# Tile 4 of both SwiGLU feed-forwards computed with seven block products in place of eight

## The chip, the cores and the metric

The kernel runs on 1 core of one Trainium2 chip. The metric is the device time of one execution in microseconds (us), lower is better. The kernel before takes 1363.11 us, the median of 3 runs (1362.15 to 1363.21).

## The reference

One hybrid decoder layer on 528 tokens (16 meta tokens and 512 of the sequence; the 112 empty ones ahead of them are masked), width 1024, in float32:

```
D_MODEL = 1024
D_FF = ((8 * D_MODEL // 3 + 127) // 128) * 128
def swiglu(x, w_in, w_out):
    a, b = jnp.split(x @ w_in, 2, axis=-1)
    return (jax.nn.silu(a) * b) @ w_out
...
    h = h + 0.5 * swiglu(rmsnorm(h, norm_ffn1), w_ffn1_in, w_ffn1_out)
    u = rmsnorm(h, norm_mix)
    fq, fk, fv, ff, rq, rk, rv, rg, ga, gb = jnp.split(u @ w_in, IN_SPLITS, axis=-1)
...
    mixed = g_a * (y_a @ w_o_fox) + g_b * (y_b @ w_o_ret)
    h = h + mixed @ w_out
    h = h + 0.5 * swiglu(rmsnorm(h, norm_ffn2), w_ffn2_in, w_ffn2_out)
```

D_FF is 2816, which is 22 inner tiles of 128 columns; each has a part a and a part b. Attention and retention, left out here, lie between the two feed-forwards.

## The kernel before, in words

Everything is kept transposed: channels on the 128 partitions, tokens along the free axis (528 in the first feed-forward, 512 in the second). A float32 product is made of three matmuls of split operands, high by high, high by low and low by high. `split` (L103) makes the two parts: ScalarE (ACT) copies the high part, VectorE (DVE) subtracts it from the source.

**The order of the feed-forward** is the string `SEQ` (L36), used twice by `ffn` (L369), once for each feed-forward. The tokens n0 and n1 are inner tiles 0 and 1, a2 b2, a3 b3 and a4 b4 are the two halves (a and b) of tiles 2, 3 and 4, each as plain products over all 1024 input channels (`mm3`, L289). From tile 5 on, e and l are the first four and the last three of seven block products, and p are the products with the output weights. The tokens u0 to u3 make sums of the normed input (`usums`, L348), on which these seven products rest: the tokens are cut into halves t1 and t2, the input channels into two halves of four chunks, the weights of a tile into a and b, and a 2 by 2 block product is made from seven products of blocks and of sums of blocks. `usums` leaves four pairs of tiles in `xa` and four in `xb`.

**TensorE (PE)** runs in the order in which the program issues (`manual_schedule`); the other engines' orders are set by a scheduler that knows priorities (`high_priority` for the epilogues of tiles below 4). All engines then run their list strictly in turn.

**A block product** (`prod`, L375) is 4 chunks of 3 matmuls, each with 264 columns in the first feed-forward and 256 in the second. With `onto=True` it adds to what its PSUM tile holds. `early` (L408) is such a use:

```
prod(b[0], w, 0, u, 0, t1)
nc.vector.tensor_tensor(cu[:, x1], b[0], R[:, t1], ALU.mult)
prod(b[1], v, 512, xa, 0, x2)
nc.vector.tensor_tensor(cu[:, x2], cu[:, x1], b[1], ALU.add)
prod(b[0], w, 512, u, 4, t1, True)
```

The third line of products adds to `b[0]`, so it can begin when DVE has read the first product out of it (L418). The four PSUM tiles of `pq` go round.

**Weights** go in pieces through `weights` (L231), four pieces ahead. A plain tile's piece (kind "w") is loaded twice by POOL's queue: once as the high part, then ACT writes its negative and a second load adds the weights to it (`ready`, L203). A tile of kind "S" is loaded whole by SP's queue into one of two raw buffers (`load`, L167); DVE makes the sums of its blocks with four operations (`wsums`, L181: L187 to L190) into the one buffer `ws`, and each piece A0, S0, A2 and S2 of raw weights or sums is split by ACT (L104) and DVE (L105).

**The epilogue** of a plain tile is `gated` (L390): three DVE operations of all tokens (L394, L397, L399), a Silu on ACT, and `store` (L384), a split. `early` and `late` have seven DVE operations of half the tokens, one of all, a Silu and `store`.

Of the kernel before, what the change touches and what calls it, by code (L numbers as in the profile page):

```python
# [19 lines left out]
AF = mybir.ActivationFunctionType  # L20
ALU = mybir.AluOpType
# [4 lines left out]
S = 512  # L26
# [6 lines left out]

SEQ = """n0 n1 a2 u0 b2 u1 a3 u2 b3 u3 a4 b4 e5 l5  # L36
          e6 p0 l6 p0 e7 p0 l7 p0 e8 p0 l8 e9 p0 l9 p0 e10 p0 l10
          e11 p1 l11 p1 e12 p1 l12 e13 p1 l13 p1 e14 p1 l14 e15 p1 l15 p1 e16 l16
          e17 p2 l17 p2 e18 p2 l18 p2 e19 p2 l19 p2 e20 p2 l20 e21 l21 p2 p3 p3 p3 p3 p3 p3 p3 p3""".split()
# [24 lines left out]
def layer(tc, order, hT, wf1i, wf1o, wf2i, wf2o, wmix, wsq, vecs, cs, rmask, rvec, cmask, outT):  # L64
    nc = tc.nc
    PSUM = bass.MemoryType.PSUM
    PE = mybir.EngineType.PE
    with ExitStack() as es:
# [18 lines left out]
        def ttile(name, dt=F32):  # L87
            return tp.tile([128, T], dt, name=name, tag="t", bufs=NT)
# [35 lines left out]
        loads = []  # L124
# [9 lines left out]
        def feed_ffn(seq, w_in, w_out):  # L134
            at_, nxt = {}, [0] * len(PJ)
            for tok in seq:
                c, j = tok[0], int(tok[1:])
                if c == "u":
                    continue
                if c == "p":  # L140
                    n = PJ[j] * 128
                    m = nxt[j]
                    nxt[j] += 1
                    if m % 2 == 0:
                        loads.append((w_out[j * 4 + m // 2], 2 * n, "w"))
                        at_[tok] = len(loads) - 1
                    pieces.append((at_[tok], m % 2 * n, n))
                    continue
                if c in "nae":
                    loads.append((w_in[j], 2048, "S" if c == "e" else "w"))  # L150
                    at_[j] = len(loads) - 1
                cuts = {"n": [0, 1024], "a": [0], "b": [1024],
                        "e": ["A0", "S0"], "l": ["A2", "S2"]}[c]
                pieces.extend((at_[j], x, 512 if x == "S2" else 1024) for x in cuts)

        feed_ffn(SEQ, wf1i, wf1o)
        for i in range((NMIX + 1) // 2):
# [5 lines left out]
        u = [], []  # L163
# [67 lines left out]
        def weights():  # L231
            i = at["u"]
            at["u"] += 1
            begin(i + 6)
            ready(i + 4)
            assert i in got
            return got.pop(i)
# [45 lines left out]
        R = cp.tile([128, T], F32, name="R")  # L283
# [85 lines left out]
        def ffn(seq, u, gain, a, pst, pq, norm, done, name):  # L369
            rng = rng_(a)  # L370
            o = po_(a)
            nh, t1, t2, x1, x2 = halves(a)
            xs = xa, xb = ([], []), ([], [])
            Rv = R[:, a:T]
            def prod(out, w, off, x, k0, ts, onto=False):  # L375


                for k in range(4):
                    c = slice(off + 128 * k, off + 128 * k + 128)
                    mm3s(out, [z[:, c] for z in w], [z[k0 + k][:, ts] for z in x], not onto and k == 0, k == 3, onto)  # L380

            g = {}

            def store(j, sv):  # L384
                xh = atile(f"{name}gh{j}", F32R)
                xl = atile(f"{name}gl{j}", F32R)
                split(xh[:, a:T], xl[:, a:T], sv)
                g[j] = xh, xl

            def gated(j, pa, pb):  # L390
                with tc.high_priority(offset=HF if j < 4 else 0):
                    sv = ttile(f"{name}s{j}")
                    for ps, x, y in pa:
                        nc.vector.tensor_tensor(sv[:, x:y], ps, R[:, x:y], ALU.mult)  # L394
                    sv = sv[:, a:T]
                    nc.scalar.activation(sv, sv, AF.Silu)
                    nc.vector.tensor_tensor(sv, sv, Rv, ALU.mult)  # L397
                    for ps, x, y in pb:
                        nc.vector.tensor_tensor(sv[:, x - a:y - a], sv[:, x - a:y - a], ps, ALU.mult)  # L399
                    store(j, sv)  # L400

            def whole(ps):
                return [(ps[:, o + a:o + T], a, T)]

            def singles(n):
                return [(pq(f"{name}{n}_{x}")[:, :y - x], x, y) for x, y in rng]

            def early(j):  # L408


                b = [pq(f"{name}q{j}_{x}")[:, :nh] for x in range(3)]
                cu = ttile(f"{name}cu{j}")[:, :2 * nh]
                d = ttile(f"{name}d{j}")[:, :nh]
                sv = ttile(f"{name}s{j}")[:, :2 * nh]
                w = weights()
                v = weights()
# [5 lines that stand above are left out]
                nc.vector.tensor_tensor(sv[:, x1], b[0], R[:, t1], ALU.mult)  # L422
                prod(b[2], v, 0, xa, 0, x1)
                nc.vector.tensor_tensor(d, cu[:, x2], b[2], ALU.add)
                return cu, d, sv

            def late(j, cu, d, sv):
                b = [pq(f"{name}r{j}_{x}")[:, :nh] for x in range(2)]
                bv = ttile(f"{name}b{j}")[:, :2 * nh]
                w = weights()  # L430
                v = weights()
                prod(b[0], w, 0, xb, 0, x1)
                nc.vector.tensor_tensor(bv[:, x2], d, b[0], ALU.add)
                prod(b[1], v, 0, u, 4, t2)
                nc.vector.tensor_tensor(sv[:, x2], b[1], R[:, t2], ALU.mult)
                nc.vector.tensor_tensor(sv[:, x2], sv[:, x2], d, ALU.add)
                nc.scalar.activation(sv, sv, AF.Silu)
                prod(b[0], w, 512, xb, 0, x2, True)
                nc.vector.tensor_tensor(bv[:, x1], cu[:, x2], b[0], ALU.add)
                nc.vector.tensor_tensor(sv, sv, bv, ALU.mult)  # L440
                return sv

            half, nxt = {}, [0] * len(PJ)
            for tok in seq:
                c, j = tok[0], int(tok[1:])
                if tok == "n0":
                    pa0, pb0 = pst(f"{name}pa0"), pst(f"{name}pb0")
                    for _ in zip(mm3(views(pa0, o, rng), weights(), u, KC), mm3(views(pb0, o, rng), weights(), u, KC)):
                        pass

                    first = []
                    for n, ps in (("sa", pa0), ("sb", pb0)):
                        sv = ttile(f"{name}{n}0")
                        nc.scalar.activation(sv[:, a:T], ps[:, o + a:o + T], AF.Copy)
                        first.append([(sv[:, a:T], a, T)])
                elif tok == "n1":
                    pa, pb = singles("pa1"), singles("pb1")
                    run(mm3(pa, weights(), u, KC))
                    norm(pa0, pb0)
                    gated(0, *first)  # L460
                    run(mm3(pb, weights(), u, KC))
                    gated(1, pa, pb)
                elif c == "u":
                    usums(j, gain, a, xs, name)
                elif c == "a":
                    half[j] = pst(f"{name}pa{j}")
                    run(mm3(views(half[j], o, rng), weights(), u, KC))
                elif c == "b":
                    pb = pst(f"{name}pb{j}")
                    run(mm3(views(pb, o, rng), weights(), u, KC))  # L470
                    gated(j, whole(half[j]), whole(pb))
                elif c == "e":
                    half[j] = early(j)
                elif c == "l":
                    store(j, late(j, *half[j]))
                else:
                    m = nxt[j]
                    nxt[j] += 1
                    js = range(sum(PJ[:j]), sum(PJ[:j + 1]))
                    x = [[g[x][i] for x in js] for i in range(2)]  # L480
                    w = weights()

                    end = a and j == len(PJ) - 1 and m == KC - 1
                    for z in ([(a, a + nh), (a + nh, T)] if end else [(a, T)]):
                        po = pst(f"{name}po{j}_{m}_{z[0]}")
                        run(mm3(views(po, o, [z] if end else rng), w, x, PJ[j]))
                        done(j, m, po[:, o + z[0]:o + z[1]], *z)
# [39 lines left out]
        u = nu  # L527
# [10 lines left out]
        with tc.tile_pool(name="psM", bufs=1, space=PSUM, reuse_waits="tile") as pM:  # L538
# [576 lines left out]
            u = [], []  # L1115
            for m in range(KC):
                x = atile(f"hh{m}")
# [130 lines left out]
```

## Time and profile before

| what | value |
|---|---|
| median of 3 runs | 1363.11 us |
| the profiled execution | 1366.41 us |
| its span, first to last instruction | 1364.3 us |
| mean granted clock of TensorE | 0.999 |
| PE busy, share of the span | 99% |
| weight loads of PE | 90% |
| DVE | 61% |
| ACT | 48% |
| POOL | 22% |
| matmuls | 8959 |
| DMA | 217.56 MB, mean 159 GB/s |

The profiled execution is one run, taken with the profiler; its span leaves out 2.1 us around the instructions. A matmul of PE is shown with its whole length though the next one starts within it, so that the distance of two starts tells what one costs. The same holds of DVE and ACT, whose next operation starts a little before the last one's end. The share of an engine over the whole span says little of one stretch.

### The profile page before, as it was taken

The numbers are of one execution on the slowest core, as the hardware profiler recorded it, in microseconds if no ns is written. First come the engines' busy times: TensorE is split into PE (matmuls) and PEld (weight loads), VectorE is DVE, ScalarE is ACT, GpSimd is POOL, SyncE is SP. The second block draws the span as 40 slices with busy tenths as digits, with TensorE's granted clock in tenths as the row PEclk, the third lists the DMA queues.
The fourth block names the chain that finished last, engine by engine and source line by source line (L and its number), as shares of the span: only waits on it lengthen the run. The fifth ranks groups of instructions, "written<-read, shape, count | busy, mean of one in ns | idle before, by whom it ended". The sixth has DMA issues, their size and how long they took to land.

```text
span 1364.3 us, 22600 instructions
## 1 busy us (share of the span) xinstructions
PE 1346.6 (99%) x8959; PEld 1229.1 (90%) x8959; DVE 836.3 (61%) x1711; ACT 657.9 (48%) x1059; POOL 300.5 (22%) x436
## 2 busy tenths in 40 slices
PE   9999999999999999999999999999999999999999
PEld 8999999999988788888888899888887999998997
DVE  6976777766455665556654565523337766777662
ACT  7433333333477677777744444453436333343331
POOL 2011111112433322333321211323421011111121
PEclk9999999999999999999999999999999999999999
DMA  9554444454996757776776766889976445555546
GB/s 295 122 143 123 127 129 118 132 143 92 288 222 140 182 130 156 169 169 149 168 179 129 149 143 141 201 228 239 268 175 124 132 131 128 134 147 133 146 90 167
DMA packets 64248, 217.56 MB, mean 159 GB/s; under 512 B 7680, under 2 KB 8064, under 8 KB 59664
## 3 DMA queue, kind: packets, MB, share of 16 engines
q0 software_dynamic: 51904, 166.91, 55.2%
q1 hardware_dynamic: 12096, 49.18, 9.9%
q8 instruction: 70, 1.15, 0.3%
q14 instruction: 34, 0.28, 0.1%
q10 hardware_dynamic: 144, 0.04, 0.0%
HBM read 207.68 MB, written 8.42 MB: 158 GB/s over the span
## 4 chain that ended last, share of the span: by engine, by line
PE 85%; issue 4%; DVE 4%; ACT 3%; POOL 2%; DMA 2%; SPq 0%; POOLq 0%; ACTq 0%
PE spo L297 9%; PE fq L307 7%; PE sq L307 7%; PE fpo L297 7%; PE pg L297 6%; PE sr L307 5%; PE fr L307 5%; PE prv L297 3%; PE oa L297 3%; PE prg L297 3%; PE ow L297 3%; PE ob L297 3%; PE pq L297 3%; PE pk L297 3%; PE fpb L297 2%
## 5 line engine op out<-in xcount | busy, mean ns | idle before, releaser
L228 ACT ACTIVATE wl<-wh 128x1024 fp32r<-128x1024 f32 (+2 forms) x169 | 160.7, 951 | 123.5 <-PE prg L297 25.0
L104 ACT ACTIVATE wh<-w 128x1024 fp32r<-128x1024 f32 (+1 forms) x74 | 76.7, 1036 | 195.7 <-issue 68.4
L104 ACT ACTIVATE wh<-ws 128x1024 fp32r<-128x1024 f32 x68 | 57.2, 841 | 99.8 <-PE fr L307 22.5
L105 DVE TENSOR_TENSOR wl<-w,wh 128x1024 fp32r<-128x1024 f32 (+1 forms) x74 | 88.0, 1189 | 6.1 <-ACT wh L104 6.1
L229 POOL DMA_DIRECT2D wl<-in_wmix x65 | 57.2, 880 | 116.4 <-ACT wl L228 98.5
L201 POOL DMA_DIRECT2D wh<-in_wmix x65 | 37.6, 579 | 183.5 <-PE pg L297 37.2
L297 PE MATMUL fpo<-fgh,wh 128*128 128x272 f32 x352 | 71.4, 284 | 0.0
L297 PE MATMUL fpo<-fgl,wh 128*128 128x272 f32 x352 | 71.3, 284 | 0.0
L297 PE MATMUL fpo<-fgh,wl 128*128 128x272 f32 x352 | 71.2, 284 | 0.0
L297 PE MATMUL spo<-sgh,wh 128*128 128x512 f32 (+1 forms) x181 | 70.2, 388 | 0.0
L297 PE MATMUL spo<-sgl,wh 128*128 128x512 f32 (+1 forms) x181 | 70.1, 387 | 0.0
L297 PE MATMUL spo<-sgh,wl 128*128 128x512 f32 (+1 forms) x181 | 70.0, 387 | 0.0
L105 DVE TENSOR_TENSOR wl<-ws,wh 128x1024 fp32r<-128x1024 f32 x68 | 64.6, 950 | 0.2 <-ACT wh L104 0.2
L105 DVE TENSOR_TENSOR pl<-PT,ph 128x512 fp32r<-128x512 f32 (+4 forms) x80 | 33.7, 432 | 48.1 <-ACT ph L104 47.6
L229 POOL DMA_DIRECT2D wl<-in_wf1o x32 | 28.2, 882 | 138.8 <-ACT wl L228 74.7
L229 POOL DMA_DIRECT2D wl<-in_wf2o x32 | 28.0, 876 | 134.9 <-ACT wl L228 70.5
L1143 DVE SCALAR_TENSOR_TENSOR hh<-spo,hh 128x512 f32<-128x512 f32 (+1 forms) x33 | 22.3, 675 | 57.8 <-PE spo L297 57.8
L297 PE MATMUL pg<-n2uh,wh 128*128 128x512 f32 x128 | 54.3, 424 | 0.0
L297 PEld LDWEIGHTS fpo<-fgh,wh 128*128 128x128 f32 x352 | 54.0, 188 | 0.0
L297 PEld LDWEIGHTS fpo<-fgl,wh 128*128 128x128 f32 x352 | 53.9, 188 | 0.0
L297 PEld LDWEIGHTS fpo<-fgh,wl 128*128 128x128 f32 x352 | 53.8, 188 | 0.0
L820 ACT ACTIVATE P<-P,st 128x144 f32<-128x144 f32 (+1 forms) x64 | 36.6, 571 | 30.7 <-DVE st L816 29.3
(959 smaller groups left out, 4665.2 us busy)
## 6 DMA issues: line engine op xcount, KB each, us to landing
wh<-in_wmix POOLq DMA_DIRECT2D x65, 512.0 KB, 4.9
wl<-in_wmix POOLq DMA_DIRECT2D x65, 512.0 KB, 7.1
w<-in_wf1i SPq DMA_DIRECT2D x18, 1024.0 KB, 7.4
w<-in_wf2i SPq DMA_DIRECT2D x17, 1024.0 KB, 7.5
wh<-in_wsq POOLq DMA_DIRECT2D x24, 512.0 KB, 5.2
wl<-in_wsq POOLq DMA_DIRECT2D x24, 512.0 KB, 7.7
wh<-in_wf1o POOLq DMA_DIRECT2D x16, 384.0 KB, 3.9
wl<-in_wf1o POOLq DMA_DIRECT2D x16, 384.0 KB, 5.3
```

What stands on the lines that cost most here:

```text
L104: nc.scalar.activation(xh, src, AF.Copy)
L105: nc.vector.tensor_tensor(xl, src, f32(xh), ALU.subtract)
L201: nc.gpsimd.dma_start(high[i][:, :w], loads[li][0][:, c:c + w])
L228: nc.scalar.activation(wl[:, :w], f32(wh[:, :w]), AF.Copy, scale=-1.0)
L229: nc.gpsimd.dma_start(wl[:, :w], raw[li][:, c:c + w], accum_op=ALU.add)
L297: nc.tensor.matmul(out, p[:, o:o + 128], q[:, a:b], start=first and k == 0 and i == 0, stop=last and k == nk - 1 and i == 2)
L307: nc.tensor.matmul(out, p, q, start=start and i == 0, stop=stop and i == 2, skip_group_check=onto)
L820: last["exp"] = nc.scalar.activation(P[i][:, :w], P[i][:, :w], AF.Exp, scale=-1.0, bias=st[:, 2:3], accum_out=sm[:, 0:1])
L1143: nc.vector.scalar_tensor_tensor(h[m][:, x:y], ps, 0.5, h[m][:, x:y], ALU.mult, ALU.add)
```

## The change

Tile 4 of both feed-forwards, computed until now by a4 and b4, becomes one token f4, with the seven block products. `foremost` issues all seven in a new order, the three that use no sums of tokens first: two of them on `u` with A0 and S2, the third with A0 again, onto `b[0]`. Then come the products with `xa` and `xb`; `b[1]` is used by three of them, the last one onto it. Tile 4's weights become kind "S" with the pieces in the order A0, S2, S0, A2. The rest of the program is as it was, but the scheduler sets the engines' orders anew.

```diff
-SEQ = """n0 n1 a2 u0 b2 u1 a3 u2 b3 u3 a4 b4 e5 l5
+SEQ = """n0 n1 a2 u0 b2 u1 a3 u2 b3 u3 f4 e5 l5
...
-                if c in "nae":
-                    loads.append((w_in[j], 2048, "S" if c == "e" else "w"))
+                if c in "naef":
+                    loads.append((w_in[j], 2048, "S" if c in "ef" else "w"))
                     at_[j] = len(loads) - 1
                 cuts = {"n": [0, 1024], "a": [0], "b": [1024],
-                        "e": ["A0", "S0"], "l": ["A2", "S2"]}[c]
+                        "e": ["A0", "S0"], "l": ["A2", "S2"], "f": ["A0", "S2", "S0", "A2"]}[c]
...
+            def foremost(j):
+
+                b = [pq(f"{name}q{j}_{x}")[:, :nh] for x in range(4)]
...
+                w = weights()
+                prod(b[0], w, 0, u, 0, t1)
+                nc.vector.tensor_tensor(cu[:, x1], b[0], R[:, t1], ALU.mult)
+                prod(b[1], weights(), 0, u, 4, t2)
+                nc.vector.tensor_tensor(sv[:, x2], b[1], R[:, t2], ALU.mult)
+                prod(b[0], w, 512, u, 4, t1, True)
+                nc.vector.tensor_tensor(sv[:, x1], b[0], R[:, t1], ALU.mult)
+                v = weights()
+                prod(b[2], v, 512, xa, 0, x2)
+                nc.vector.tensor_tensor(cu[:, x2], cu[:, x1], b[2], ALU.add)
+                w = weights()
+                prod(b[1], w, 0, xb, 0, x1)
+                bv = ttile(f"{name}b{j}")[:, :2 * nh]
+                nc.vector.tensor_tensor(bv[:, x2], cu[:, x2], b[1], ALU.add)
+                prod(b[3], v, 0, xa, 0, x1)
+                nc.vector.tensor_tensor(d, cu[:, x2], b[3], ALU.add)
+                nc.vector.tensor_tensor(bv[:, x2], bv[:, x2], b[3], ALU.add)
+                nc.vector.tensor_tensor(sv[:, x2], sv[:, x2], d, ALU.add)
+                nc.scalar.activation(sv, sv, AF.Silu)
+                prod(b[1], w, 512, xb, 0, x2, True)
+                nc.vector.tensor_tensor(bv[:, x1], cu[:, x2], b[1], ALU.add)
+                nc.vector.tensor_tensor(sv, sv, bv, ALU.mult)
+                return sv
...
+                elif c == "f":
+                    store(j, foremost(j))
```

Where the order of DVE changes. In the kernel before, this stands on DVE ahead of the first read of a block product (the last row, tile 5 of the first feed-forward; `fs_903` is tile 4's epilogue, `ws_924` the sums of tile 6's weights):

```order
L394 TENSOR_TENSOR fs_903<-fpa_797,R 128x528
L105 TENSOR_TENSOR wl_919<-ws_714,wh_798 128x512
L187 TENSOR_TENSOR ws_924<-w_712 128x512
L397 TENSOR_TENSOR fs_903<-fs_903,R 128x528
L188 TENSOR_TENSOR ws_924<-ws_924,w_712 128x512
L189 TENSOR_TENSOR w_712<-w_712 128x512
L190 TENSOR_TENSOR ws_924<-w_712,ws_924 128x512
L399 TENSOR_TENSOR fs_903<-fs_903,fpb_850 128x528
L105 TENSOR_TENSOR wl_929<-w_712,wh_851 128x1024
L105 TENSOR_TENSOR fgl_909<-fs_903,fgh_908 128x528
L418 TENSOR_TENSOR fcu_915<-fq_0_912,R 128x264
```

In the changed kernel the first read of a block product is that of tile 4, and tile 5's weights have their sums made right behind it (`fxbl_792` is the last of what u3 makes; `ws_822` are the sums of tile 5, `fq_0_795` and `fq_1_796` are `b[0]` and `b[1]` of tile 4):

```order
L105 TENSOR_TENSOR wl_803<-w_422,wh_645 128x1024
L105 TENSOR_TENSOR fxbl_792<-fxb_782,fxbh_791 128x528
L451 TENSOR_TENSOR fcu_799<-fq_0_795,R 128x264
L187 TENSOR_TENSOR ws_822<-w_559 128x512
L105 TENSOR_TENSOR wl_827<-w_559,wh_716 128x1024
L188 TENSOR_TENSOR ws_822<-ws_822,w_559 128x512
L189 TENSOR_TENSOR w_559<-w_559 128x512
L190 TENSOR_TENSOR ws_822<-w_559,ws_822 128x512
L453 TENSOR_TENSOR fs_801<-fq_1_796,R 128x264
L455 TENSOR_TENSOR fs_801<-fq_0_795,R 128x264
```

The first read of `b[0]` stands directly behind the whole of u3, and the read of `b[1]` (L453) behind the four sums and one split of tile 5's weights. Further on, this stands on DVE between tile 4's last product and tile 5's first read (`ws_937` are the sums of tile 6, `fgl_922` is tile 4's `store`):

```order
L466 TENSOR_TENSOR fs_801<-fs_801,fd_800 128x264
L105 TENSOR_TENSOR wl_932<-ws_822,wh_856 128x512
L469 TENSOR_TENSOR fb_889<-fcu_799,fq_1_796 128x264
L187 TENSOR_TENSOR ws_937<-w_820 128x512
L470 TENSOR_TENSOR fs_801<-fs_801,fb_889 128x528
L188 TENSOR_TENSOR ws_937<-ws_937,w_820 128x512
L189 TENSOR_TENSOR w_820<-w_820 128x512
L105 TENSOR_TENSOR fgl_922<-fs_801,fgh_921 128x528
L190 TENSOR_TENSOR ws_937<-w_820,ws_937 128x512
L105 TENSOR_TENSOR wl_942<-w_820,wh_873 128x1024
L418 TENSOR_TENSOR fcu_928<-fq_0_925,R 128x264
```

Tile 6's sums, tile 4's last two operations with its `store`, and the split of tile 6's first piece now stand between tile 4's last read of `b[1]` (L469) and tile 5's first read (L418); before, one split and one `store` stood between tile 4's last operation (L399) and that read.

## Rows read from the trace of the kernel before

**Rows 1.** The page, part 1: busy time, share of the span, instructions.
```profile
PE 1346.6 (99%) x8959; PEld 1229.1 (90%) x8959; DVE 836.3 (61%) x1711; ACT 657.9 (48%) x1059; POOL 300.5 (22%) x436
```

**Rows 2.** Windows: length, busy PE, PEld, DVE, ACT, POOL; granted clock; DMA.
```profile
44.00:56.00 12.00, 12.00 (x101) 12.00 (x101) 12.00 (x22) 5.35 (x8) 0.88 (x1) 1.00 0.28 46
446.20:449.60 3.40, 3.40 (x11) 2.73 (x10) 2.79 (x5) 2.35 (x5) 1.53 (x3) 0.50 0.92 217
1045.00:1057.00 12.00, 12.00 (x53) 9.72 (x52) 11.86 (x22) 4.94 (x8) 0.42 (x1) 1.00 0.12 24
```

**Rows 3.** Waits of PE: us in total, times, longest us.
```profile
PE k2pm L661 <- ACT k2sh L104: 2.1, 1, 2.1
PE sq L307 <- DVE scu L418: 1.6, 1, 1.6
PE fq L307 <- DVE fcu L418: 1.4, 1, 1.4
```

**Rows 4.** Timeline of PE, both feed-forwards: start, length, what.
```profile
56.23 0.41 PE L297 MATMUL fpa<-n1uh,wh 128*128 128x272 f32 x2
...
67.91 0.28 PE L307 MATMUL fq<-n1uh,wh 128*128 128x264 f32 x1
...
69.37 0.29 PE L307 MATMUL fq<-fxah,wh 128*128 128x264 f32 x1
...
70.96 0.39 PE L307 MATMUL fq<-n1uh,wh 128*128 128x264 f32 x1
...
1056.34 0.40 PE L297 MATMUL spa<-n3uh,wh 128*128 128x512 f32 x1
...
1067.50 0.29 PE L307 MATMUL sq<-n3uh,wh 128*128 128x256 f32 x1
...
1068.93 0.28 PE L307 MATMUL sq<-sxah,wh 128*128 128x256 f32 x1
...
1070.52 0.39 PE L307 MATMUL sq<-n3uh,wh 128*128 128x256 f32 x1
```

**Rows 5.** Timeline of DVE, first feed-forward.
```profile
32.24 0.71 DVE L394 TENSOR_TENSOR fs<-fsa,R 128x528 f32<-128x528 f32 x1
...
39.08 0.71 DVE L105 TENSOR_TENSOR fgl<-fs,fgh 128x528 fp32r<-128x528 f32 x1 [1.21 <-ACT fgh L104]
...
56.05 0.77 DVE L355 SCALAR_TENSOR_TENSOR fbk<-h,VEC,R 128x528 f32<-128x528 f32 x1
56.73 0.43 DVE L358 TENSOR_TENSOR fxa<-fbc 128x264 f32<-128x264 f32 x1
57.08 0.43 DVE L360 TENSOR_TENSOR fxb<-fbk,fbc 128x264 f32<-128x264 f32 x1
...
57.77 1.22 DVE L105 TENSOR_TENSOR wl<-ws,wh 128x1024 fp32r<-128x1024 f32 x1
58.90 0.70 DVE L399 TENSOR_TENSOR fs<-fs,fpb 128x528 f32<-128x528 f32 x1
59.52 0.43 DVE L361 TENSOR_TENSOR fxb<-fbk,fxa 128x264 f32<-128x264 f32 x1
...
70.48 0.43 DVE L418 TENSOR_TENSOR fcu<-fq,R 128x264 f32<-128x264 f32 x1
```

**Rows 6.** Timeline of DVE, second feed-forward.
```profile
1033.36 0.69 DVE L394 TENSOR_TENSOR ss<-ssa,R 128x512 f32<-128x512 f32 x1
...
1053.13 0.69 DVE L105 TENSOR_TENSOR sxbl<-sxb,sxbh 128x512 fp32r<-128x512 f32 x1
1053.73 1.22 DVE L105 TENSOR_TENSOR wl<-w,wh 128x1024 fp32r<-128x1024 f32 x1
1054.87 0.74 DVE L355 SCALAR_TENSOR_TENSOR sbc<-hh,VEC,R 128x512 f32<-128x512 f32 x1
1055.53 0.74 DVE L355 SCALAR_TENSOR_TENSOR sbk<-hh,VEC,R 128x512 f32<-128x512 f32 x1
```

**Rows 7.** The page, part 6: DMA issues, KB each, us to landing.
```profile
w<-in_wf1i SPq DMA_DIRECT2D x18, 1024.0 KB, 7.4
```

More of the change, by code (lines that the diff above doesn't have):

```diff
@@ L441, in late @@
                 return sv
+            def foremost(j):
+                b = [pq(f"{name}q{j}_{x}")[:, :nh] for x in range(4)]
+                cu = ttile(f"{name}cu{j}")[:, :2 * nh]
+                d = ttile(f"{name}d{j}")[:, :nh]
+                sv = ttile(f"{name}s{j}")[:, :2 * nh]
+                w = weights()
[21 more added lines that the diff above has]
+                return sv
             half, nxt = {}, [0] * len(PJ)
```

## The prediction

> **What bounds the kernel now.** I read the page's shares first: PE is busy 99% of the span and DVE 61% [rows 1]. So a us in which PE stands is a us of the result, and matmuls saved are us saved, as long as PE is fed. Then the windows around the place: in both feed-forwards DVE is as full as PE there, 12.00 of 12 us in the first and 11.86 in the second [rows 2], because u0 to u3 are made there beside the epilogues of tiles 0 to 3. ACT has 5.35 and 4.94 of 12 us to do. Last the waits of PE: one of 1.4 and one of 1.6 us already come from exactly the read that the change puts there, L418, which takes a block product out of its PSUM tile before the next product adds to it [rows 3]. So the question is not how many matmuls go, but when DVE gets to these reads.
>
> **What PE saves.** In the first feed-forward a4 begins at 56.23 us and tile 5 at 67.91: tile 4 takes 11.68 us. A product takes 69.37 - 67.91 = 1.46 us; seven are 10.22, so 1.46 are saved. In the second: 1067.50 - 1056.34 = 11.16; a product takes 1.43, with the start that I round to 1.42; seven are 9.94, so 1.22 are saved [rows 4]. Together 2.68 us, if PE waits for nothing.
>
> **What DVE gets to do.** Cost per operation, start to start [rows 5]: 0.68 us for L355 (56.05 to 56.73), 0.345 for half the tokens, 1.14 for a split of 1024 (57.77 to 58.90), 0.62 for all tokens (58.90 to 59.52). In the second [rows 6]: 0.60 for 512, 1.14, and 0.66 for L355; 0.34 for 256. Per tile 4 the change adds to DVE three and a half splits of weights (3 x 1.14 + 0.60 = 4.0 us) and four sums (2.4), which POOL's loads did so far; its epilogue goes from three operations of all tokens to eight of half and one of all, 1.6 us more. It takes nothing away from DVE. ACT exchanges two casts of 1024 for four splits: in the windows above it has the time, so nothing. SP loads 1 MB more for each feed-forward, POOL four pieces fewer.
>
> **The first read.** Product 2 takes `b[1]`, product 3 adds to `b[0]`, so it must wait until L451 has read `b[0]`. In the order shown with the change, L451 stands behind all of u3. From the first operation after the norm (L394 at 32.24 [rows 5]) DVE has ahead of it: 22 operations of all tokens (8 splits in `usums`, 14 of epilogues), two pairs of pieces of tile 1 at 0.68 a pair, 8 of L355, 16 of half, three splits of 1024 and one of 512 of tile 4's weights. That is 13.64 + 1.36 + 5.44 + 5.52 + 3.42 + 0.60 = 29.98 us, so L451 starts at 62.22. It takes 0.43, and 0.05 later PE can go on (before: a read at 70.48 of 0.43, PE at 70.96 [rows 4, 5]): 62.70. PE is done with products 1 and 2 at 56.23 + 2.92 = 59.15. **Wait 3.55 us.**
>
> **The next two.** Product 4 needs no new buffer; PE ends it at 65.62. Product 5 overwrites `b[1]`, whose read L453 stands behind L451, one sum, one split of 1024 and three more sums: 62.22 + 0.345 + 0.60 + 1.14 + 1.80 = 66.10, and 0.48 later PE starts, at 66.58. **Wait 0.96.** Product 6 ends at 69.50. Product 7 adds to `b[1]` behind L462; up to it DVE has three halves and two splits of 1024, 3.32 us, so it starts at 69.42 and PE at 69.90. **Wait 0.40.** Product 7 ends at 71.36.
>
> **The wait in tile 5.** Tile 5's third product adds to its `b[0]` behind L418. L469 can start with the end of product 7's last matmul, 71.24 + 0.28 = 71.52; then DVE has, as the last order shown says, 0.345, one sum, L470, two sums, the split of the `store`, a sum and a split of 1024: 5.12 us. L418 starts at 76.65, PE at 77.13. Two products after 71.36 PE would be there at 74.28. **Wait 2.85.** Before, this product started at 70.96 [rows 4]. So the first feed-forward loses 77.13 - 70.96 = **6.17 us**, and from there on DVE keeps up as before: nothing is added to later tiles.
>
> **The second feed-forward**, by the same steps from 1033.36 [rows 6]: 24 operations of 512 (the last split of u3 stands behind the read here), 8 of L355, 16 of 256, three splits: 14.52 + 5.28 + 5.41 + 3.42 = 28.63; read at 1061.99, PE on at 1062.46 instead of 1059.18: wait 3.28. L453 at 1066.47, behind that split too; product 5 at 1066.94 instead of 1065.30: 1.64. Product 7 at 1070.24 instead of 1069.78: 0.46; its end 1071.66. L469 at 1071.82, 5.08 us to L418, PE at 1077.37 instead of 1074.50: 2.87. Before, it was 1070.52 [rows 4]: **6.85 us** lost. Sum of both: **13.0 us**.
>
> **The clock.** [...] Bounds: 0, and 0.3 + 1.7 + 1.7 = 3.7 us. I take 1.7, one stretch that counts, since one row at 2.1 us shows that it happens and none that it must.
>
> [...]
>
> **What is covered.** Tile 6's weights are loaded into the raw buffer of tile 4, free when A2 is split at about 61.6 us; 7.4 us later [rows 7] they are there, 69.0, and their first sum is due at 71.9. That cover is 2.9 us; a load later than that would move L418 by as much.
>
> **Sum.** 13.0 + 1.7 = 14.7 us. The profiled execution took 1366.41 us with a span of 1364.3; it would take 1381.1 and 1379.0. The median of the runs shown is 3.3 us lower, so the forecast is 1363.11 + 14.7 = **1377.8 us**. A measurement of this kernel tells about 0.2%, 2.7 us, from no change.
>
> **The rivals.** *PE decides* (4%): the seven products go through without a wait, and 2.7 us are saved: 1360.4. For it speaks that PE is the fullest engine [rows 1]. It decides if L451 could start by 58.7, 3.5 us sooner than I count; against it, DVE had no free time in which to catch up [rows 2].
> [...]
>
> *Only tile 4 waits* (10%): DVE reaches L418 in time, because the scheduler's queue of 5.1 us meets operands that are there, and the 2.85 and 2.87 are not paid: 13.0 - 5.7 = 7.3, 1370.4 us. It would need DVE to save 2.9 of 5.1 us; nothing in the rows is that much faster.
>
> *More than the walk* (10%): ACT's splits come late. Before, DVE stood for one of them for 1.21 us at 39.08 [rows 5]; if each feed-forward loses 1 us more in this way and the clock its 3.7, it is 13.0 + 2.0 + 3.7 = 18.7: 1381.8. Against it: the casts of tile 4's pieces (L228), for which ACT has to await POOL's loads, are among what the change takes away.
>
> *Nothing to be seen* (4%): PE's waits are half of what I count, and the saving meets them: 1363 to 1366.
>
> **The numbers.** The forecast's own case has 72%, 1376.1 (no clock) to 1379.8 (all of it). With the second and third rival the range is 1370.4 to 1381.8 and leaves out some 8%, and as much again for what the walk misses. Faster 0.04, same 0.04, slower 0.92.
>
> **What would show it.** PE's waits for L451 and L453 of 3 to 4 and 1 to 2 us in each feed-forward, and for L418 in tile 5 of about 2.9; PE at 98% or less; DVE without a gap from 40 to 71 us; tile 6 beginning about 6 and 13 us later than before; half clock after some of these waits. I am wrong if the third product of tile 4 starts right after the second, or if L418 in tile 5 isn't waited for.

## The result, and the profile after

The changed kernel takes **1380.76 us**, the median of 3 runs (1377.57 to 1382.90), against 1363.11: 17.7 us more, a ratio of 1.0123 with a 95% interval of 1.0108 to 1.0139. The profiled execution is the fastest of the three, 1377.57 us with a span of 1375.7; the other two had spans of 1378.8 and 1381.0 at mean granted clocks of 0.995 and 0.993 instead of 0.998.

Part 1 of the page after, the line that answers to [rows 1]:

```profile
PE 1345.6 (98%) x8983; PEld 1230.3 (89%) x8983; DVE 852.5 (62%) x1741; ACT 661.8 (48%) x1063; POOL 296.3 (22%) x428
```

PE is busy 1.0 us less than before, a smaller share of a longer span; DVE is busy 16.2 us more. Where PE stood, by its waits (us in total, times, longest), beside [rows 3]:

```profile
PE sq L307 <- DVE scu L418: 4.4, 2, 2.8
PE fq L307 <- DVE fcu L418: 4.3, 2, 2.9
PE fq L307 <- DVE fcu L451: 3.7, 1, 3.7
PE sq L307 <- DVE scu L451: 3.4, 1, 3.4
...
PE k2pm L693 <- ACT k2sh L104: 1.4, 1, 1.4
```

`fq` is a product's PSUM tile in the first feed-forward, `sq` in the second. Four waits are new: for L451 at tile 4 and for L418 at tile 5, each once in both. The smaller waits for L418 of before (1.4 and 1.6) are still in the totals: they stand at a much later tile, at 249 and 1243 us of the kernel before. Tile 5's read was not waited for there. The two in the first feed-forward, in PE's timeline (start, us, operation, in brackets the idle time ahead and what ended it):

```profile
63.08 0.42 PE L307 MATMUL fq<-n1uh,wh 128*128 128x264 f32 x1 [3.67 <-DVE fcu L451]
...
77.99 0.40 PE L307 MATMUL fq<-n1uh,wh 128*128 128x264 f32 x1 [2.89 <-DVE fcu L418]
```

DVE meanwhile, in its timeline; [rows 5] are its operations in the same place before. No idle time stands in a bracket until the fourth row, and it is the only one between 42 and 78 us:

```profile
62.60 0.42 DVE L451 TENSOR_TENSOR fcu<-fq,R 128x264 f32<-128x264 f32 x1
...
66.49 0.42 DVE L453 TENSOR_TENSOR fs<-fq,R 128x264 f32<-128x264 f32 x1
...
69.78 0.42 DVE L462 TENSOR_TENSOR fb<-fcu,fq 128x264 f32<-128x264 f32 x1
...
70.75 0.43 DVE L464 TENSOR_TENSOR fd<-fcu,fq 128x264 f32<-128x264 f32 x1 [0.56 <-PE fq L307]
...
77.51 0.43 DVE L418 TENSOR_TENSOR fcu<-fq,R 128x264 f32<-128x264 f32 x1
```

And the clock, in windows (their length, then PE, PEld, DVE, ACT and POOL busy, then the granted clock, the DMA share and GB/s):

```profile
56.00:60.00 4.00, 3.41 (x29) 3.20 (x27) 4.00 (x9) 1.26 (x2) 0.00 (x0) 1.00 0.00 0
60.00:64.00 4.00, 0.92 (x5) 0.92 (x6) 4.00 (x7) 0.67 (x2) 0.00 (x0) 0.91 0.21 49
64.00:68.00 4.00, 4.00 (x24) 4.00 (x24) 4.00 (x7) 2.53 (x3) 0.56 (x1) 0.66 0.63 247
68.00:72.00 4.00, 4.00 (x35) 4.00 (x34) 3.44 (x8) 1.10 (x2) 0.00 (x0) 1.00 0.49 124
...
76.00:80.00 4.00, 2.01 (x16) 2.01 (x17) 2.60 (x5) 0.00 (x0) 0.00 (x0) 1.00 0.00 0
80.00:86.00 6.00, 6.00 (x51) 6.00 (x50) 3.94 (x8) 2.43 (x3) 1.68 (x3) 1.00 0.40 86
...
1064.00:1068.00 4.00, 0.97 (x4) 0.98 (x5) 4.00 (x8) 1.26 (x2) 0.00 (x0) 0.85 0.24 70
1068.00:1072.00 4.00, 4.00 (x26) 3.84 (x25) 4.00 (x8) 2.00 (x3) 0.55 (x1) 0.72 0.56 222
```

From 60 to 64 us PE ran 5 matmuls, from 64 to 68 it ran 24 where 35 is usual: half clock, right behind the wait. A second such stretch follows the wait for L451 at 1067. None follows the two waits for L418: the clock is 1.00 from 76 to 86 us, and from 1080 to 1088. Tile 6 of the first feed-forward begins at 85.42 instead of 78.38, 7.0 us late; in the second the lateness grows from 4.3 to 11.6, by 7.3. Between them 3.5 us come back at 446: PE's wait for ACT is 1.4 there instead of 2.1 [rows 3], a wait of 0.8 for DVE ahead of it is gone, and so is the half-clock stretch of before [rows 2], with a clock of 1.00 from 440 to 460 us; 0.8 go to a wait for ACT ahead of that (`pff`, 1.1 instead of 0.3). 7.0 + 0.8 - 3.5 + 7.3 = 11.6, close to the 11.4 by which the profiled spans differ.

### The profile page after: what moved, and what is told of

It reads as the page before. It is cut to its first block, busy times and chain, and to the rows that moved or that the text cites. A ratio compares the mean times of both kernels' runs of the same rounds, so it can differ in the third digit from the quotient of the medians.

```text
span 1375.7 us, 22681 instructions
## 1 busy us (share of the span) xinstructions
PE 1345.6 (98%) x8983; PEld 1230.3 (89%) x8983; DVE 852.5 (62%) x1741; ACT 661.8 (48%) x1063; POOL 296.3 (22%) x428
## 4 chain that ended last, share of the span: by engine, by line
PE 78%; DVE 9%; ACT 5%; issue 4%; DMA 2%; POOL 1%; SPq 0%; POOLq 0%; ACTq 0%; DVEq 0%
PE spo L297 9%; PE fq L307 7%; PE sq L307 7%; PE fpo L297 7%; PE pg L297 5%; PE sr L307 5%; PE fr L307 5%; PE prv L297 3%; PE oa L297 3%; PE prg L297 3%; PE ow L297 3%; PE ob L297 3%; PE pq L297 3%; PE pk L297 3%; PE prk L297 2%
## 5 line engine op out<-in xcount | busy, mean ns | idle before, releaser
L228 ACT ACTIVATE wl<-wh 128x1024 fp32r<-128x1024 f32 (+2 forms) x165 | 156.5, 949 | 115.4 <-PE prg L297 25.0
L104 ACT ACTIVATE wh<-w 128x1024 fp32r<-128x1024 f32 (+1 forms) x78 | 80.9, 1038 | 197.6 <-issue 68.7
L104 ACT ACTIVATE wh<-ws 128x1024 fp32r<-128x1024 f32 (+1 forms) x72 | 60.6, 842 | 104.3 <-PE fr L307 21.4
L105 DVE TENSOR_TENSOR wl<-w,wh 128x1024 fp32r<-128x1024 f32 (+1 forms) x78 | 92.9, 1191 | 6.2 <-ACT wh L104 6.2
L105 DVE TENSOR_TENSOR wl<-ws,wh 128x1024 fp32r<-128x1024 f32 (+1 forms) x72 | 68.4, 950 | 0.2 <-ACT wh L104 0.2
L201 POOL DMA_DIRECT2D wh<-in_wf1o x32 | 19.9, 622 | 148.6 <-PE fq L307 68.3
```

Source lines behind the costliest of these rows:

```text
L104: nc.scalar.activation(xh, src, AF.Copy)
L105: nc.vector.tensor_tensor(xl, src, f32(xh), ALU.subtract)
L201: nc.gpsimd.dma_start(high[i][:, :w], loads[li][0][:, c:c + w])
L228: nc.scalar.activation(wl[:, :w], f32(wh[:, :w]), AF.Copy, scale=-1.0)
```

## The experiments

Theory 1 is the prediction's: DVE has more to do ahead of the reads than it has time for, and PE stands until it gets there. Rival 2: the reads only stand badly in DVE's list. Rival 3: PE itself (matmuls, weights). Rival 4: the clock. Each run's time stands beside runs of the kernel before on the same chip.

**One feed-forward at a time.** The token f4 is put back to a4 b4 in the second, then in the first:

```diff
+SEQB = " ".join(SEQ).replace("f4", "a4 b4").split()
-        feed_ffn(SEQ, wf2i, wf2o)
+        feed_ffn(SEQB, wf2i, wf2o)
...
-            ffn(SEQ, u, gn2, NM, psB, pqB, norm2, done2, "s")
+            ffn(SEQB, u, gn2, NM, psB, pqB, norm2, done2, "s")
```

> The first feed-forward has f4, the second a4 b4 as before. Theory 1 (DVE has more to do than it has time for ahead of the reads of tile 4 and 5, and PE waits for it): in the changed kernel tile 6 of the first feed-forward began 85.42 - 78.38 = 7.0 us later, 3.5 of which were given back at 446 us, where a half-clock stretch of before is gone; so 3.5 to 7 us above the kernel before, 1366.6 to 1370.2 us, and the first feed-forward's waits as in the changed kernel (L451 3.7, L418 2.9 us). Rival (the two places share a cause outside them, such as the loads of weights or PE's clock over the whole span): most of the 17.7 us or next to nothing of them.

> The second feed-forward has f4, the first a4 b4 as before. Theory 1: the changed kernel's second tile 5 ended 7.3 us later than before by itself (4.26 to 11.56 us in the shift of PE), so 1370.4 us, give or take 2, with waits of 3.4 (L451) and 2.8 us (L418) there and the first feed-forward as before. What this run and the one with the first alone lose should add up to the loss of the changed kernel, 17.7 us, within 4. Rival (a shared cause): they do not add up.

The first alone: 1370.83 against 1363.85 us, 1.0051 (1.0036 to 1.0066). The second alone: 1371.09, 1.0063 (1.0046 to 1.0079). That is 7.0 and 7.2, together 14.2 of 17.7, within the 4 allowed. The first is 0.6 us above the top of its expectation (1370.2, reckoned from 1363.11; the runs of the kernel before beside it are 0.7 higher). The two places lose apart from each other, and each shows its own two waits (3.7 and 2.9, 3.4 and 2.8).

**DVE's new work alone, on the eight products of before.**

```diff
-                    loads.append((w_in[j], 2048, "S" if c == "e" else "w"))
+                    loads.append((w_in[j], 2048, "S" if c == "e" or tok == "a4" else "w"))
...
+                cuts = {"a4": ["A0", "S2", "S0"], "b4": ["A2"]}.get(tok, cuts)
...
+                    if j == 4:
+                        weights()
+                        weights()
```

(One of the sums, which would overwrite raw weights, goes to a place that nothing uses.)

> The kernel before, with a4 and b4 as plain products of eight, but tile 4's weights come as in the change: SP loads them whole, DVE makes the four sums and ACT and DVE split all four pieces (two of the pieces are used by nothing). So DVE has 4.0 + 2.4 = 6.4 us more per feed-forward ahead of tile 5's first read (L418), and PE's products, their order and the epilogue are those of before. Theory 1: L418 comes up to 6.4 us later, its wait grows from 1.4 and 1.6 to 6 or 8 us, and the time by 9 to 13 us: 1372 to 1376, with half clock after each wait up to 1379. Rival 2 (it is where the new reads stand, products that add to a PSUM tile soon after another's end, and not what DVE has to do): 1362 to 1366. Rival 3 (PE or the weights' loads): nothing above 1366 either.

1376.19 against 1363.85 us: **+12.3**, 1.0097 (1.0079 to 1.0115). PE runs the matmuls of before, 8959, and yet (L422 is L418 of before; the totals hold the later tile's 1.4 and 1.6):

```profile
PE sq L311 <- DVE scu L422: 6.8, 2, 5.2
PE fq L311 <- DVE fcu L422: 5.8, 2, 4.4
```

New waits of 4.4 and 5.2 us at tile 5, with half clock behind both (0.65 from 74 to 78 us, 0.50 from 1076 to 1080), under the 6 to 8 expected. That expectation added to waits of 1.4 and 1.6 that do not stand at tile 5; and of the 6.4 us some 2 went into idle time that DVE had before, 1.21 at 39.08 [rows 5] and 0.8 between 62 and 70 us, in the second feed-forward 1.1 at 1068. DVE has no idle time in this run from 42 us up to the read. Rivals 2 and 3 cannot make this loss: no product was moved and none is new. This is the main finding: the way in which tile 4's weights are made costs 12.3 us by itself, with the half clock behind its waits and without the saving of the seven products.

**The order of the reads alone.**

```diff
-                nc.vector.tensor_tensor(cu[:, x1], b[0], R[:, t1], ALU.mult)
+                with tc.high_priority(offset=60):
+                    nc.vector.tensor_tensor(cu[:, x1], b[0], R[:, t1], ALU.mult)
```

and so for L453 and for tile 5's L418.

> The changed kernel with the reads L451, L453 and tile 5's L418 given a higher priority: DVE's list has the same operations, these reads sooner. Theory 1: DVE has no less to do, so the waits for L451 and L453 get shorter and what was passed over (the sums of u3 that products 4 to 7 need, weights' sums and splits) is late instead; from 1370 to 1380 us. Rival 2 (the order alone): the waits of 3.4 to 3.7 and 2.8 to 2.9 us are gone and none comes in their place, 13 us less than the changed kernel, 1360 to 1366. Rival 4 (the clock alone): as the changed kernel, 1378 to 1383.

1376.35 us, 1.0091 (1.0073 to 1.0110). The waits moved on to a read that was passed over, L465 (L462 of the change):

```profile
PE sq L307 <- DVE sb L465: 4.0, 1, 4.0
PE fq L307 <- DVE fb L465: 4.0, 1, 4.0
```

Some 4 to 5 us better than the changed kernel (the two intervals just touch), as theory 1 had it, and not 13.

**PE kept busy in the waits.**

```diff
+            def busy(what, n):
+                z = pst(f"{name}z{what}")
+                for _ in range(n):
+                    nc.tensor.matmul(z[:, :512], bones, u[0][0][:, a:a + 512], start=True, stop=True)
```

> The changed kernel with matmuls added whose result nothing uses: 14 of 512 columns ahead of tile 4's third product and 12 ahead of tile 5's third, in both feed-forwards, which at the 0.23 us of such a matmul fill 3.2 and 2.8 us, about the waits for L451 (3.7 and 3.4) and L418 (2.9 and 2.8). DVE and the order of the rest are unchanged. Theory 1 (DVE holds PE; the clock is a small part that differs between runs): the reads come when they came, PE goes on when it did, and only the half-clock stretches go: 1374 to 1379 us, with the single runs closer together than the 5.3 us of the changed kernel. Rival 4 (the loss is mostly a clock that falls in the waits): 1368 or less. Rival 3 (PE's own work bounds it there): 11 to 12 us longer than the changed kernel, 1390.

1377.44 against 1364.63 us: **+12.8**, 1.0099 (1.0084 to 1.0114); the four runs lie within 1.8 us, and the granted clock around both places is 1.00 in every window. So what DVE holds PE up for costs 12.8 without any half clock there. At full clock the wait for the next read shows as well (L460 is L453 of the change):

```profile
PE sq L307 <- DVE ss L460: 1.4, 1, 1.4
...
PE fq L307 <- DVE fs L460: 0.7, 1, 0.7
```

The changed kernel's 17.7 has about 5 us more, but not from the two stretches of its trace: tile 6 begins at 85.39 and 1089.21 us here, at 85.42 and 1089.33 there. Of the 5 us, 3.3 lie between the medians, as the changed kernel's other two runs were 3.2 and 5.3 us longer than the traced one, and 1.5 between the kernels before on the two chips; the intervals of the two ratios just overlap.

**ACT takes the reads.**

```diff
-                nc.vector.tensor_tensor(cu[:, x1], b[0], R[:, t1], ALU.mult)
+                nc.scalar.activation(cu[:, x1], b[0], AF.Copy)
+                nc.vector.tensor_tensor(cu[:, x1], cu[:, x1], R[:, t1], ALU.mult)
```

and so for L453, L462 and tile 5's L418.

> The changed kernel, but ACT copies the first three of tile 4's products that are waited for (L451, L453, L462) and tile 5's first (L418) out of PSUM, and DVE multiplies or adds from SBUF later. DVE has no operation less, ACT four more. Rival 2 (only these reads stand badly): PE's waits for them go and with them 13 us or more: 1360 to 1366. Theory 1 (DVE has too much to do there): the waits for these reads go, but the next thing of DVE's that PE needs (later reads, splits of weights, the sums of u3) is late and takes part of it back: half to two thirds of the loss stays, 1368 to 1376.

1373.13 us, 1.0065 (1.0049 to 1.0081), +8.5. PE now waits 1.9 and 2.8 us for the next read of tile 5, which DVE still does (L426 there), besides smaller ones. About half of the loss stays, though DVE no longer holds up these reads; the other half went with them.

**Work given to GpSimd.** In the first of two runs L397 and the store's subtraction of tiles 0 to 3, and the sums of tiles 5 and 6:

```diff
-                    nc.vector.tensor_tensor(sv, sv, Rv, ALU.mult)
+                    (nc.gpsimd if j < 4 else nc.vector).tensor_tensor(sv, sv, Rv, ALU.mult)
...
+            en = nc.gpsimd if st["n"] % 18 in (1, 2) else nc.vector
```

> The changed kernel with work taken from DVE and given to GpSimd, which is busy 22%: in the epilogues of tiles 0 to 3 the multiplication L397 and the subtraction of the store's split, and the sums of tile 5's and tile 6's weights (L187 to L190). That takes 4 x 2 x 0.62 + 2.4 = 7.4 us per feed-forward from DVE ahead of tile 5's L418, and no read is moved or changed. Theory 1: that is more than the waits for L451 and L418 together (6.5 us), so nearly the whole loss goes: 1360 to 1367 us. Rival 2 (the order of the reads, not the amount): over 1372. If GpSimd's longer operations (about 1.4 us for 128x512 in the rows of before) are late themselves, the waits are for GpSimd and the time lies between.

> Both: ACT copies the reads that PE waits for out of PSUM, and GpSimd takes L397 and the store's subtraction of tiles 0 to 3 and the sums of tile 5's weights from DVE. Theory 1: no wait for DVE over 1 us is left at tiles 4 and 5, those for L418 that the kernel before had (1.4 and 1.6 us) go too, and the seven products save their 2.7 us: 1358 to 1363 us, at or under the kernel before. Rival 3 (the seven products cost PE something that no wait shows): above 1366.

Both expectations were missed by far: 1392.13 us, 1.0201 (1.0184 to 1.0218), and with ACT's copies (and the sums of tile 5 alone) 1384.94, 1.0152 (1.0137 to 1.0168). DVE's list is shorter, but its sums of half the tokens took 1.48 to 1.52 us while GpSimd computed, against 0.42. DVE's timeline of the first run (L360 to L363 are L358 to L361 of before, and the L397 shown is L394 of before):

```profile
57.37 0.69 DVE L397 TENSOR_TENSOR fs<-fpa,R 128x528 f32<-128x528 f32 x1
...
60.80 1.50 DVE L360 TENSOR_TENSOR fxa<-fbc 128x264 f32<-128x264 f32 x1
62.23 1.48 DVE L362 TENSOR_TENSOR fxb<-fbk,fbc 128x264 f32<-128x264 f32 x1
...
66.21 0.42 DVE L363 TENSOR_TENSOR fxb<-fbk,fxa 128x264 f32<-128x264 f32 x1
```

and GpSimd's at the same time:

```profile
56.85 1.75 POOL L189 TENSOR_TENSOR ws<-w 128x512 f32<-128x512 f32 x1
58.68 1.63 POOL L190 TENSOR_TENSOR ws<-ws,w 128x512 f32<-128x512 f32 x1
60.28 1.73 POOL L191 TENSOR_TENSOR w<-w 128x512 f32<-128x512 f32 x1
...
69.42 1.54 POOL L390 TENSOR_TENSOR fgl<-fs,fgh 128x528 fp32r<-128x528 f32 x1 [4.56 <-ACT fgh L389]
```

A sum of half the tokens takes 0.42 us at 66.21, where GpSimd is idle (the 4.56 us ahead of 69.42), and 1.5 beside its sums, nearly one operation of GpSimd for one of DVE. The L397 at 57.37, one operand of which comes from PSUM, kept its 0.69. At times GpSimd seems to be the one held up: an operation like the one at 69.42 is shown with 4.88 us from 52.00 on, and DVE's sums kept their 0.42 there up to 55. PE's first wait at tile 4 grew to 9.9 us.

**Work given to ACT and the DMA engines.** First the pieces A0 and A2 of tiles 4 to 6, then the same with ACT's copies:

```diff
+                elif li in viad and c in ('A0', 'A2'):
+                    o = 512 * int(c[1])
+                    nc.scalar.activation(wl[:, :w], f32(wh[:, :w]), AF.Copy, scale=-1.0)
+                    nc.gpsimd.dma_start(wl[:, :w], loads[li][0][:, o:o + w], accum_op=ALU.add)
```

In both runs A2 carries a raw block of the weights in place of the difference that the sums (L189) write over it; the number and size of the operations do not hang on that.

> The changed kernel, with the raw pieces A0 and A2 of tiles 4, 5 and 6 made as the plain tiles' are (loaded by POOL's queue, ACT writes the negative, a second load adds), so that DVE has six splits of 1024 less per feed-forward and GpSimd computes nothing. Two of them (tile 4's, 2.28 us) stand ahead of L451, one (tile 5's A0) ahead of L453 and one (tile 6's A0) ahead of tile 5's L418. No read is moved, no read changed. Theory 1 (DVE's amount of work): L451's waits fall from 3.7 and 3.4 to about 1.4 and 1.1 us, that for L453 goes, L418's fall by about 1 to 1.8; 2 x (2.3 + 1 + 1) = 8.6 us less than the changed kernel, without half clock 1366 to 1369, at most 1372. Rival 2 (the order of the reads): the waits stay, 1376 or more. A third theory, from the runs with GpSimd (any work beside DVE slows DVE): DVE's operations get longer and the time stays above 1376 as well.

> As the run before, and ACT copies the reads that PE waits for (L451, L453, L462, tile 5's L418) out of PSUM as in the run with ACT's copies. Theory 1: with 6.8 us less of DVE's work per feed-forward and the reads off its list, no wait of PE for DVE over 1 us is left at tiles 4 and 5; the seven products save their 2.7 us, and the waits of 1.4 and 1.6 us that the kernel before had for L418 go as well: 1358 to 1362 us, 0.996 to 0.999 of the kernel before. If something costs time in the seven products that the waits don't show, 1364 or more.

1377.33 us, 1.0099 (1.0076 to 1.0122), and 1373.22, 1.0075 (1.0061 to 1.0088): both missed. The first is in the time that rival 2 had, but its waits are not those: PE's waits for DVE fell where theory 1 had them fall (in the first of the two runs L451's in the second feed-forward from 3.4 to 0.9 us, both for L418 to 1.8), but the wait for L451 in the first feed-forward grew from 3.7 to 4.6. There, what was taken from DVE came back as idle time, 3.48 us in the first run:

```profile
41.11 0.71 DVE L105 TENSOR_TENSOR fgl<-fs,fgh 128x528 fp32r<-128x528 f32 x1 [3.48 <-ACT fgh L104]
```

ACT's operation was late as ACT stood behind a cast of tile 4's A0 (L231), and that one for its load:

```profile
38.97 1.06 ACT L231 ACTIVATE wl<-wh 128x1024 fp32r<-128x1024 f32 x1 [4.54 <-DMA wh<-in_wf1i]
```

The DMA share is 1.08 and 1.07 there, from 34 to 42 us: the DMA engines were full. They were so in the kernel before (1.09 and 1.07), where DVE stood for 1.21 us in this place [rows 5]. In the second run PE's long waits at tiles 4 and 5 were for ACT (3.0 us) and for a load (2.8).

**The same where the DMA engines have time.** Tile 4's weights stay on DVE; the low parts of the stores of tiles 0 to 4 and A0 of tiles 5 and 6 go to ACT and POOL's queue. With ACT's copies, and without:

```diff
+                if j in (0, 1, 2, 3, 4):
+                    nc.scalar.activation(xh[:, a:T], sv, AF.Copy)
+                    nc.scalar.activation(xl[:, a:T], f32(xh[:, a:T]), AF.Copy, scale=-1.0)
+                    nc.gpsimd.dma_start(xl[:, a:T], sv, accum_op=ALU.add)
```

> The changed kernel; ACT copies the reads that PE waits for (L451, L453, L462, tile 5's L418) out of PSUM as in the run with ACT's copies, and DVE has fewer operations without GpSimd computing: the low parts of the stores of tiles 0 to 4 and of the raw piece A0 of tiles 5 and 6 are made as the plain tiles' weights are (ACT writes the negative of the high part, a load of POOL's queue adds the source). Tile 4's weights, whose loads met full DMA engines from 30 to 42 us in the last two runs, stay on DVE. DVE loses 4 x 0.62 = 2.5 us ahead of L451 and 0.62 + 2 x 1.14 = 2.9 us more ahead of tile 5's L418. Theory 1 (DVE's amount of work): with 5.4 us less per feed-forward, the 8.5 us that the run with ACT's copies lost go too and the seven products begin to pay: 1360 to 1365 us, 0.998 to 1.001 of the kernel before. If the new loads come late (DMA contention, as in the last two runs), PE's or DVE's waits are for DMA and the time lies between 1366 and 1374.

> As the run before, but every read out of PSUM stays on DVE as in the changed kernel: only DVE's amount of work is smaller, by 2.5 us ahead of L451, by 1.1 more ahead of L453 and by 1.8 more ahead of tile 5's L418 in each feed-forward. Theory 1 (amount): L451's waits fall from 3.7 and 3.4 us to 1 or 1.5, L418's from 2.9 and 2.8 to 1 or 1.5; 7 to 10 us less than the changed kernel with the half clock that goes: 1367 to 1372 us. Rival 2 (the order of the reads): the time stays at that of the changed kernel, 1376 or more.

With ACT's copies 1366.34 against 1363.48 us, 1.0021 (1.0011 to 1.0030), above the 1360 to 1365 expected. Its profiled run was the slowest of its eleven, 1371.84, with waits of 1.9 us for ACT in the first feed-forward, where the DMA engines were full again ahead of it (a share of 1.03 and 1.08 from 62 to 70 us), and of 2.7 for the load of tile 5's A0 in the second. Without them 1367.40 against 1364.14, 1.0022 (1.0013 to 1.0031), within its expectation, with every read on DVE as in the change. Its waits of tile 4 and 5 (L466 is L451, L433 is L418, L477 is L462; the totals for L433 hold the later tile's 1.4 and 1.6):

```profile
PE sq L317 <- DVE scu L433: 2.6, 2, 1.6
PE fq L317 <- DVE fcu L433: 2.4, 2, 1.4
...
PE sq L317 <- DVE scu L466: 1.4, 1, 1.4
...
PE sq L317 <- DVE sb L477: 0.7, 1, 0.7
PE fq L317 <- DVE fb L477: 0.6, 1, 0.6
```

Taking 5.4 us of DVE's work away in each feed-forward gives back 14.4 of 17.7 us (17.7 - 3.3), and its clock is 1.000 in the profiled run. So the amount of DVE's work is enough to explain the loss. Where the reads stand counts only while DVE is full: sooner in its list they gave back 4 to 5 us, copied by ACT 9; ACT's copies add nothing once DVE has the time (1.0021 and 1.0022). No version here beats the kernel before; the best is 0.2% slower.

## Why the prediction was right

The direction, the place and the mechanism were right: 1377.8 forecast, 1380.76 measured, inside 1370.4 to 1381.8. That it is inside is in part luck: it lies above 1379.8, where the forecast's own case ended, in the room that was left for late ACT splits, which the trace does not show. By its steps:

- **What PE saves**, 2.68 us: not to be seen by itself, but consistent. In the last run an undisturbed product takes the 1.46 us counted (61.12 to 62.58), and the new waits (0.2, 0.6, 1.0 and 1.4, 1.0, 0.7) are 4.9 us; less 2.7 that is 2.2. By PE's starts tile 6 comes 0.9 us late in the first feed-forward and 2.3 more in the second, 3.2 together, with 3.3 measured. So by my estimate from these six a wait costs some 0.2 us more than its idle time, which is counted only from the end of the last matmul (one of 0.28 us in the trace, where the next starts after 0.12).
- **The first read**: L451 forecast at 62.22, seen at 62.60; the wait 3.55 forecast, 3.67 seen, and 3.28 against 3.41 in the second. The walk through DVE's list was better than that: from L394 to L451 it took 30.03 and 28.59 us, with 29.98 and 28.63 forecast; the 0.4 us came before it, as L394 began at 32.57 instead of 32.24. The two waits of [rows 3] that the prediction took as signs of this read stand at 249 and 1243 us, far from it; the sum does not use them.
- **The next two** waits, 0.96 and 0.40, 1.64 and 0.46, did not show up as such in the changed kernel: L453 came at 66.49, 0.4 late, but PE, at half clock (0.66 from 64 to 68), needed that time for products 3 and 4 itself. In the run with PE kept busy, at full clock, PE starts product 5 0.87 and 1.54 us late behind L453 and product 7 0.25 and 0.30 late behind L462: the four waits were there.
- **The wait in tile 5**: 2.85 and 2.87 forecast, 2.89 and 2.76 seen, at 77.51 instead of 76.65.
- **The sum without the clock**, 13.0: the run with PE kept busy measured 12.8, the runs of one feed-forward 14.2 together with their half clock.
- **The clock** is the term that stays open. No run shows the 1.7 us that the sum adds for it, nor the bound of 3.7, as a loss of the change: they were my estimate, from the 3.4 us at a granted clock of 0.50 in the kernel before [rows 2]. The traced run shows two stretches, both after L451 (0.66 from 64 to 68 us, 0.72 from 1068 to 1072), in time in which PE would have waited for the next reads anyway, and none after L418 (1.00 from 76 to 86 and from 1080 to 1088); with PE kept busy tile 6 began only 0.03 and 0.12 us sooner. So the clock cost next to nothing there, and the traced run is 14.5 us above the median of before (1377.57 - 1363.11), where 14.7 was forecast. What the forecast does not count is that the stretch at 446 us can go as well (1.00 from 440 to 460 in the traced run), and that runs differ: the two others had lower clocks and were 3.2 and 5.3 us longer. Where their stretches lay is open, since only one run has a trace; and the interval of the ratio makes the 17.7 itself 14.7 to 18.9.
- **The upper end of the forecast's own case**, 1379.8 us, takes the whole 3.7 for the clock, my estimate. The median is nearer to that than to my 1377.8; yet in the trace two of four waits, of 2.9 and 2.8 us, were followed by a clock of 1.00, and before one of 2.1 by 0.50 [rows 2, 3].
- **Rivals.** "PE decides" was wrong by the waits, and "only tile 4 waits" by L418's 2.9. "More than the walk" would have been nearest in time, 1381.8, but by late ACT splits, which the trace does not show.
- **A miscount** without effect: tile 4's epilogue has nine operations of half the tokens, not eight, and `early` and `late` together have eight, not seven; the walk names its operations one by one and does not use these totals.

## What to carry to other kernels

An engine at 61% of the span can be the bound of the stretch that a change touches (DVE was busy 12.00 of 12 us there [rows 2]): read its windows there, then walk its list from the last point at which it was idle up to the operation that the next engine waits for, with start-to-start times. Here a product saved on PE, 1.2 to 1.5 us, was bought with 6.4 us of sums and splits on a full DVE. And before work is moved to a free engine, look at what the full one and the loads do beside it: with GpSimd's sums running, DVE's of half the tokens took 1.5 us instead of 0.42, and new loads met DMA engines at a share of 1.03 to 1.08. Keeping the clock up gained only 0.03 and 0.12 us up to tile 6 here, where PE had to wait for the next reads anyway.

## What was not expected of the hardware

DVE's sums of half the tokens, from SBUF to SBUF, went from 0.42 to 1.5 us while GpSimd computed beside them, so that with work taken away from DVE the loss against the kernel before rose from 17.7 to 27.5 us, where less work taken away in another manner brought it to 3.3. And PE's clock fell behind waits of 5.2, 4.4, 3.7 and 3.4 us (to 0.50, 0.65, 0.66 and 0.72 in windows of 4 us), but not behind 2.9 and 2.8 (1.00); in the first run with loads for the splits it fell behind one of 1.8 (0.64 from 78 to 82 us). PE's wait of 2.1 us for ACT near 446 was followed by half clock in the kernel before (0.50) and by full clock in the last run, whose mean is 1.000: the length of a wait alone did not tell.
